# Gate and up products of a SwiGLU as seven half-size block products, with weight sums made by adding transfers

## The chip, the cores and the metric

The kernel runs on one core of a Trainium2 chip. The metric is the device time of one launch, in microseconds (us). Before the change three runs took 2916.46, 2917.67 and 2917.93 us; the median is 2917.67 us. The engines are named as the profile names them: PE (TensorE matmuls), PEld (its weight loads), DVE (VectorE), ACT (ScalarE), POOL (GpSimd) and SP (SyncE, which here only issues transfers).

## The reference

One encoder layer on 512 tokens of width 2048. A token mixer is followed by a layer norm, then by the part that the change touches:

```
h = x * (1.0 + sc_f) + sh_f                                   # x: the normed first residual, 512 x 2048
y = (silu(h @ w_gate) * (h @ w_up)) @ w_down                  # w_gate, w_up: 2048 x 5632; w_down: 5632 x 2048
x = layer_norm(ALPHA * x + (1.0 + gt_f) * y, ln2_g, ln2_b)
```

All of it is float32.

## The kernel before

Activations that feed a product stand feature-major: 128 features on the partitions, 512 tokens along a row. Every float32 product is three passes in float32r. An operand is cut into hi (rounded by an ACT copy) and lo = x - hi (a DVE subtraction), and `mm3` issues hi*hi, hi*lo and lo*hi into one PSUM bank. A weight tile of 128 x 1024 therefore costs an ACT copy (`round_to`, L319) and a DVE subtraction (`split_to`, L331). Five raw tiles (NRAW) and four hi/lo pairs (NW) are in rotation; the weights come from DRAM as one stream of such tiles in the order of use, loaded by SP.

The second half of the program, in order:

- The products with w_out give y, token tile by token tile for the last 512 columns. DVE makes the residual z in SBUF (`t0_0` to `t3_3`) and its statistics. `finish1(t)` norms a token tile, transposes it on PE (bank `zt`), scales it on ACT to h (tile `h2`), and DVE writes hi and lo of h (`m_hi`, `m_lo`).
- 44 feature tiles f of 128 features each. `gate_up` takes for each f a gate and an up product over 16 feature tiles of h: 16 x 3 matmuls of 512 columns each. The first feature tile is cut in two halves of 256 tokens, so that the last token tile can be normed meanwhile.
- After each part of four feature tiles, `down` multiplies the part before with w_down and DVE adds the result to `yacc`, which begins as ALPHA (z g + b) made on POOL (`base_side`).
- The last part goes by token tile, with the second layer norm behind it.

The order is written out by hand in each engine's own program order. Generators in `side` add the small work, one step for every 12 matmuls. Each engine runs its rows in order and waits where an operand is not there.

Of the kernel before, what the change touches and what calls it, by code (L numbers as in the profile page):

```python
# [13 lines left out]
"""  # L14
# [14 lines left out]
P = 128  # L29
D = 2048  # L30
# [26 lines left out]
NHEAP = 38  # L57
NSMALL = 14
# [12 lines left out]
def stream_keys():  # L71
    """The weight tiles in the order in which the products use them."""
# [28 lines left out]
    def gu(p):  # L101
        return [(g, f, i) for f in range(p * PART, p * PART + PART) for g in ("gate", "up") for i in range(2)]

    def down(p):
        return [("down", f, c) for c in range(4) for f in range(p * PART, p * PART + PART, 2)]

    ks += gu(0)
    for p in range(1, NPART):
        ks += gu(p) + down(p - 1)
# [3 lines left out]
    ks += [k for k in down(NPART - 1) if not k[2]] + stay  # L113
    return ks
# [3 lines left out]
def layer_kernel(ctx, tc, ws, wa, wada, xt, x, cin, bada, lbl, ghg, gcq, gckv, ln1c, lnrow, ident, lvm, dist, out):  # L118
# [6 lines left out]
    hp = ctx.enter_context(tc.tile_pool(name="heap", bufs=NHEAP))  # L125
# [6 lines left out]

    def big(name, dt=FR):
        return bp.tile([P, 4, T], dt, name=name, tag="big")
# [4 lines left out]
    # ---------------------------------------------------------------- constants  # L139
# [18 lines left out]
    # cond = silu(c) on every partition  # L158
# [64 lines left out]
    keys = stream_keys()  # L223
# [25 lines left out]
    class Stream:  # L249
        def __init__(self):  # L250
# [20 lines left out]
        def load_to(self, e):  # L271
            """Load at least up to this entry, and as far as the room reaches."""
            while self.ndma < len(entries):
                kind = entries[self.ndma]
                pool, most = self.room(kind)
                if self.ndma >= e and sum(self.room(entries[n])[0] == pool for n in self.raw) >= most:
                    break
# [6 lines left out]
                if kind[0] == "w":  # L284
                    nc.sync.dma_start(r, ws[kind[1]])
# [10 lines left out]
        def round_to(self, goal):  # L296
            """Take the adaLN products, round the weight tiles to hi, up to this entry of the stream."""
            while self.nhi <= min(goal, len(entries) - 1):
                e = self.nhi
                self.load_to(e + 1)  # L300
                kind = entries[e]
# [4 lines left out]
                else:  # L306
                    r = self.raw[e]
                    key = keys[kind[1]] if kind[0] == "w" else kind
# [16 lines left out]
        def split_to(self, goal):  # L325
            """The rests lo = w - hi, up to this entry."""
            self.round_to(goal)
            while self.nlo <= min(goal, len(entries) - 1):
# [10 lines left out]
        def get(self, *key, ahead=2):  # L339
            """A weight tile; the next ones that pass through are prepared ahead."""  # L340
            at = place_of["w", keys.index(key)]
            goals = [at]
            for e in range(at + 1, len(entries)):
                if len(goals) > ahead:
                    break
                if entries[e][0] == "w" and keys[entries[e][1]] not in self.held:
                    goals.append(e)
            if len(goals) <= ahead and not any(e[0] == "w" and keys[e[1]] not in self.held for e in entries[at + 1:]):
                goals.append(len(entries) - 1)
# [3 lines left out]
            return self.ready.pop(entries[at])  # L353

    W = Stream()

    # ---------------------------------------------------------------- h = x (1 + sc_m) + sh_m, its narrow projections
# [13 lines left out]
    def keep(key, ps):  # L371
        """Partial sums over the first features leave the banks."""
# [23 lines left out]
    def lower_bounds():  # L396
        """softmax over depth, cumsum - p0"""
# [17 lines left out]
    for k in range(KD):  # L415
# [37 lines left out]
        if k in (1, 2):  # L453
            # values of two token tiles over the first features
# [12 lines left out]
    # ---------------------------------------------------------------- rms of c_q and c_kv, spilled for the attention  # L467
# [29 lines left out]
    # ---------------------------------------------------------------- the indexer: scores and the 128 largest per query  # L497
# [5 lines left out]
    def key_side(t):  # L503
        """Index keys on both halves of the partitions; index weights token-major."""
# [13 lines left out]
    def index_queries(ps, h):  # L518
        """hi and lo of a head's index queries, one on each half of the rows, so that one product takes both."""
# [65 lines left out]
    # ---------------------------------------------------------------- token-major projections v, silu(g) for four heads  # L585
# [38 lines left out]
    def plus(res, ps, part):  # L624
        """res = ps + part"""
# [124 lines left out]
    # ---------------------------------------------------------------- sigmoid gates of the merge, spilled  # L750
# [56 lines left out]
    for j in range(4, KD):  # L807
        if j == 12:
# [3 lines left out]
            # the first 128 tokens unsplit: latent queries of two heads, latent keys  # L812
# [7 lines left out]
    # ---------------------------------------------------------------- attention: values of all heads, token-major  # L820
    # hi and lo of a head side by side, so that one product takes both
# [15 lines left out]
    # head pipeline: latent queries of head h, softmax of head h-1, values of head h-2  # L837
# [14 lines left out]
    def at_scores(h):  # L852
        """The products of a head's scores, up to the last query tile and then that; its softmax."""
# [66 lines left out]
    # y_a comes back while the last heads run; its products fill the end of the head pipeline  # L920
# [95 lines left out]
    # the residual gates scale the columns of w_out and w_down before these are split  # L1016
# [10 lines left out]
    # tiles that stay: the end of w_out and of w_down is taken token tile by token tile  # L1027
    def hold_out():
        return [(heap("wohi", FR), heap("wolo", FR)) for _ in range(2)]
# [4 lines left out]
    last_w = {}  # L1034

    def hold_down(f, c):
        def place():
            if c not in last_w:
                last_w[c] = (big(f"wdhi{c}"), big(f"wdlo{c}"))
            n = f - (NF - PART)  # L1040
            return [tuple(t[:, n + i] for t in last_w[c]) for i in range(2)]
        return place

    for c in range(1, 4):
        for f in range(NF - PART, NF, 2):
            W.held["down", f, c] = hold_down(f, c)

    # ---------------------------------------------------------------- merged = sig(ga) (y_a w_pa) + sig(gb) (y_b w_pb)
# [13 lines left out]
    del yb_hi, yb_lo, sa, sb  # L1062

# [335 lines left out]
```

## Time and profile before

| | |
|---|---|
| median of three runs | 2917.67 us |
| profiled execution: first to last instruction | 2914.7 us (the page gives no other time of it) |
| PE busy | 2874.3 us, 99% |
| DVE, ACT, POOL busy | 1664.9, 865.0, 382.3 us |
| end of the w_out products, start of gate and up | 1455.6 us |
| bytes moved by transfers | 407.46 MB, 140 GB/s on the mean |

The profile page sums each engine's busy time; a chain of waits follows the work that ended last back to the start; window tables give the same sums for one stretch. Matmuls overlap their neighbours, so the rate of PE is read from how far apart a run of them starts and not from the length of one.

### The profile page before, as it was taken

The numbers are of one execution on the slowest core, as the hardware profiler recorded it, in microseconds if no ns is written. First come the engines' busy times: TensorE is split into PE (matmuls) and PEld (weight loads), VectorE is DVE, ScalarE is ACT, GpSimd is POOL, SyncE is SP. The second block draws the span as 40 slices with busy tenths as digits, with TensorE's granted clock in tenths as the row PEclk, the third lists the DMA queues.
The fourth block names the chain that finished last, engine by engine and source line by source line (L and its number), as shares of the span: only waits on it lengthen the run. The fifth ranks groups of instructions, "written<-read, shape, count | busy, mean of one in ns | idle before, by whom it ended". The sixth has DMA issues, their size and how long they took to land.

```text
span 2914.7 us, 33709 instructions
## 1 busy us (share of the span) xinstructions
PE 2874.3 (99%) x13226; PEld 2391.8 (82%) x13226; DVE 1664.9 (57%) x2429; ACT 865.0 (30%) x1276; POOL 382.3 (13%) x435
## 2 busy tenths in 40 slices
PE   8999999999999999999999999999999999999997
PEld 6878888888888888888888888888888888888885
DVE  7877777778834876456643534244343524344358
ACT  4334342333223554222332222222222222222221
POOL 1011223332012443000062000000000000000003
PEclk9999999999999999999999999999999999999998
DMA  9866455557952124444233322332332233232341
GB/s 387 329 203 190 154 170 175 177 174 261 315 194 95 51 73 169 149 137 130 75 121 101 102 96 92 101 100 88 102 100 96 93 102 99 89 101 97 105 132 65
DMA packets 116049, 407.46 MB, mean 140 GB/s; under 512 B 14225, under 2 KB 14529, under 8 KB 112817
## 3 DMA queue, kind: packets, MB, share of 16 engines
q1 hardware_dynamic: 104690, 369.35, 37.7%
q0 software_dynamic: 10912, 35.64, 3.8%
q8 instruction: 104, 1.70, 0.2%
q14 instruction: 55, 0.45, 0.1%
q10 hardware_dynamic: 288, 0.31, 0.0%
HBM read 386.62 MB, written 16.27 MB: 138 GB/s over the span
## 4 chain that ended last, share of the span: by engine, by line
PE 94%; DVE 3%; DMA 1%; issue 1%; ACT 0%; POOL 0%; SPq 0%; DVEq 0%; POOLq 0%; ACTq 0%
PE gate L204 16%; PE up L204 16%; PE dn L204 16%; PE y L204 6%; PE gb L204 6%; PE ga L204 6%; PE qb L204 3%; PE pb L204 3%; PE g L204 3%; PE v L204 3%; PE pa L204 2%; PE early L204 2%; PE s L204 2%; PE a L204 1%; PE q L204 1%; PE f L204 1%
## 5 line engine op out<-in xcount | busy, mean ns | idle before, releaser
L331 DVE TENSOR_TENSOR wlo<-raw,whi 128x1024 fp32r<-128x1024 f32 (+1 forms) x486 | 597.2, 1251 | 474.4 <-ACT whi L319 470.2
L319 ACT ACTIVATE whi<-raw 128x1024 fp32r<-128x1024 f32 (+1 forms) x486 | 498.7, 1047 | 514.0 <-DVE raw L1022 241.3
L204 PE MATMUL gate<-mhi,wlo 128*128 128x512 f32 (+1 forms) x720 | 276.8, 384 | 0.0
L204 PE MATMUL up<-mhi,wlo 128*128 128x512 f32 (+1 forms) x720 | 276.8, 384 | 0.0
L204 PE MATMUL gate<-mlo,whi 128*128 128x512 f32 (+1 forms) x720 | 276.7, 384 | 0.0
L204 PE MATMUL gate<-mhi,whi 128*128 128x512 f32 (+1 forms) x720 | 276.7, 384 | 0.0
L204 PE MATMUL up<-mlo,whi 128*128 128x512 f32 (+1 forms) x720 | 276.7, 384 | 0.0
L204 PE MATMUL up<-mhi,whi 128*128 128x512 f32 (+1 forms) x720 | 276.7, 384 | 0.0
L204 PE MATMUL dn<-whi,gthi 128*128 128x512 f32 x656 | 255.2, 389 | 0.0
L204 PE MATMUL dn<-wlo,gthi 128*128 128x512 f32 x656 | 255.2, 389 | 0.0
L204 PE MATMUL dn<-whi,gtlo 128*128 128x512 f32 x656 | 255.2, 389 | 0.0
L1209 DVE TENSOR_TENSOR t<-t,dn 128x512 f32<-128x512 f32 x160 | 106.5, 684 | 141.2 <-PE dn L204 140.2
L1190 DVE TENSOR_TENSOR silu<-silu,up 128x512 f32<-128x512 f32 x43 | 29.6, 687 | 271.3 <-PE up L204 271.3
L1253 POOL DMA_DIRECT2D l<-in_lnrow x8 | 4.3, 542 | 1299.0 <-PE dn L204 1212.4
L204 PEld LDWEIGHTS gate<-mlo,whi 128*128 128x128 f32 x720 | 135.3, 188 | 26.9
L204 PEld LDWEIGHTS gate<-mhi,whi 128*128 128x128 f32 x720 | 135.3, 188 | 26.8
L204 PEld LDWEIGHTS up<-mlo,whi 128*128 128x128 f32 x720 | 135.3, 188 | 26.8
L204 PEld LDWEIGHTS up<-mhi,whi 128*128 128x128 f32 x720 | 135.3, 188 | 26.8
L204 PEld LDWEIGHTS gate<-mhi,wlo 128*128 128x128 f32 x720 | 135.3, 188 | 26.8
L204 PEld LDWEIGHTS up<-mhi,wlo 128*128 128x128 f32 x720 | 135.3, 188 | 26.8
L204 PEld LDWEIGHTS dn<-whi,gthi 128*128 128x128 f32 x656 | 123.1, 188 | 25.6
L204 PEld LDWEIGHTS dn<-wlo,gthi 128*128 128x128 f32 x656 | 123.1, 188 | 25.6
(349 smaller groups left out, 5672.2 us busy)
## 6 DMA issues: line engine op xcount, KB each, us to landing
raw<-in_ws SPq DMA_DIRECT2D x480, 512.0 KB, 3.9
raw<-in_wada SPq DMA_DIRECT2D x128, 512.0 KB, 4.9
rawb<-in_wada SPq DMA_DIRECT2D x22, 1024.0 KB, 12.1
raws<-in_wada SPq DMA_DIRECT2D x40, 256.0 KB, 6.3
d_gate<-sgate POOLq DMA_DIRECT2D x32, 256.0 KB, 3.0
raw<-in_wa SPq DMA_DIRECT2D x16, 384.0 KB, 10.0
raws<-in_xt SPq DMA_DIRECT2D x16, 256.0 KB, 10.3
spa<-d_gate POOLq DMA_DIRECT2D x16, 256.0 KB, 3.1
```

What stands on the lines that cost most here:

```text
L204: mmul(*a, **k)
L319: nc.scalar.activation(hi, src, AF.Copy)
L331: nc.vector.tensor_sub(lo, src, hi.bitcast(FT))
L1190: nc.vector.tensor_mul(s, s, ps)
L1209: nc.vector.tensor_add(yacc[t][c], yacc[t][c], ps)
L1253: nc.gpsimd.dma_start(rows2[n][c], lnrow[2 + n][:, c * T:c * T + T].to_broadcast([P, T]))
```

## The change

Gate and up become block products. The weight matrix is cut into four blocks (two halves of the features f, two halves of the 2048 inputs), h into four (two halves of the inputs, two of the tokens). A pair of feature tiles p and p + 22 of one kind (a "quad", 44 in all) is computed by seven products of half size in place of eight, in the Winograd form. Each is 8 x 3 matmuls of 256 columns (`product`). Three of them use plain blocks of h, four use sums of blocks: R5, R7, R6, R4.

- The sums of h are made once: `block_sums` adds or subtracts on DVE, `put` writes hi by ACT and lo by DVE. `sums_side` does this for R7, R6 and R4, R5 goes into `m_hi` and `m_lo`. The order of the first products is changed so that four plain ones run first.
- The sums of weights are made by transfers that add what they bring to what lies in the SBUF tile (`accum_op=OP.add`), issued by POOL: four for each quad, beside four plain loads by SP. Each state of a raw tile is split by ACT and DVE for its product (`prepare`, three steps ahead of PE): seven splits where there were four.
- The results are combined out of PSUM by ACT copies and DVE adds (`use`), and silu(gate) * up goes to DRAM (`d_g`).
- w_down is a stage of its own behind all gate and up products; its activations come back from DRAM and are split (`g_tiles`). z goes to DRAM as well (`d_z`), comes back for the first norm of the last columns, and again for `base_side`, which now runs beside w_down.

```
-    def gate_up(p, skip=0):
...
-                        mm3(ps, whi[:, w], wlo[:, w], *mh(k), k == 0, k == KD - 1)
...
+SEVEN = ("p1", "q5", "p2", "q7", "r6", "q4", "p3")
...
+    seq = [(0, "p1"), (1, "p1"), (0, "p2"), (1, "p2")]
+    seq += [(n, i) for n in range(2) for i in SEVEN if i not in ("p1", "p2")]
+    seq += [(n, i) for n in range(2, len(QUADS)) for i in SEVEN]
...
+        for step, what in ((s - 4, "F1"), (s - 3, "F3"), (s - 2, "+F1"), (s - 1, "Z"), (s + 2, "Y")):
...
+    BLOCK = {"F1": (1, 0), "F3": (0, 0), "Z": (0, 1), "Y": (1, 1), "+F1": (1, 1)}
+    OF = {"q5": "F1", "r6": "F1", "p1": "F3", "q7": "F3", "p2": "Z", "p3": "Z", "q4": "Y"}
...
+    def fetch_for(step):
+        for n, what in fetch.pop(step, ()):
+            if what[0] == "+":
+                nc.gpsimd.dma_start(raws[n, what[1:]], block(n, what), accum_op=OP.add)
...
+            nc.sync.dma_start(r, block(n, what))
...
+    def prepare(step):
+        fetch_for(step)
...
+        split(r, hi, lo)
+        if i == "q5":
+            nc.gpsimd.dma_start(r, block(n, "F3"), accum_op=OP.add)
+        elif i == "p1":
+            nc.gpsimd.dma_start(r, block(n, "F1"), accum_op=OP.add)
+        if i == ("p2" if n > 1 else "q5"):
+            nc.gpsimd.dma_start(raws[n, "Z"], raws[n, "F1"], accum_op=OP.add)
...
+    def put(v, hi, lo):
+        nc.scalar.activation(hi, v, AF.Copy)
+        nc.vector.tensor_sub(lo, v, hi.bitcast(FT))
...
+        for c in range(2):
+            r = passing("r5")
+            nc.vector.tensor_sub(r, hraw[t - 2, c], hraw[t, c])
+            put(r, m_hi[c][:, :, s], m_lo[c][:, :, s])
+        yield "R5"
...
+    def product(step):
+        for k in range(8):
+            mm3(ps, whi[:, w], wlo[:, w], *factor(i, k), fresh and k == 0, k == 7, f=mmul, skip_group_check=True)
...
+    for step in range(4, len(seq)):
+            prepare(step + 3)
+        product(step)
+        use(step)
```

DVE where gate and up begin: before, `h` is the last token tile of h on its way into `mhi` and `mlo`, and `wlo` are weight rests.

```order
L1106 TENSOR_TENSOR mlo0_9438<-h2_11801,mhi0_9437 128x4x128
L1105 CAST mhi1_9723<-h2_11808 128x4x128
L1106 TENSOR_TENSOR mlo1_9724<-h2_11808,mhi1_9723 128x4x128
L1105 CAST mhi2_10009<-h2_11837 128x4x128
L1106 TENSOR_TENSOR mlo2_10010<-h2_11837,mhi2_10009 128x4x128
L1105 CAST mhi3_10295<-h2_11844 128x4x128
L1106 TENSOR_TENSOR mlo3_10296<-h2_11844,mhi3_10295 128x4x128
L331 TENSOR_TENSOR wlo_11940<-raw_11364,whi_11939 128x1024
```

The same place on DVE now, from the last lo of R7 to the weight rest behind R4:

```order
L1142 TENSOR_TENSOR R7_1_11962<-h2_11898,R7_1_11962 128x4x128
L1157 TENSOR_TENSOR h2_11582<-h2_11893,h2_11582 128x512
L1157 TENSOR_TENSOR h2_11589<-h2_11898,h2_11589 128x512
L1142 TENSOR_TENSOR R6_0_11963<-h2row_11410,R6_0_11963 128x4x128
L1142 TENSOR_TENSOR R6_1_11964<-h2row_11410,R6_1_11964 128x4x128
L1142 TENSOR_TENSOR R6_0_11963<-h2_11582,R6_0_11963 128x4x128
L1142 TENSOR_TENSOR R6_1_11964<-h2_11589,R6_1_11964 128x4x128
L273 TENSOR_TENSOR wlo_11986<-raw_11806,whi_11985 128x1024
L1160 TENSOR_TENSOR h2_11546<-h2_11546,h2_11582 128x512
L1160 TENSOR_TENSOR h2_11553<-h2_11553,h2_11589 128x512
L1142 TENSOR_TENSOR R4_0_11965<-h2row_11410,R4_0_11965 128x4x128
```

Behind the last token tile DVE had only weight rests; now the sums of h stand between them, six rows for each of R7, R6 and R4.

POOL in the first 100 us of gate and up, before: the rows of the second layer norm's base.

```order
L1165 DMA ln0_3_12026<-in_lnrow 128x512
L1166 TENSOR_SCALAR ln0_3_12026<-ln0_3_12026 128x512
L1165 DMA ln1_3_12030<-in_lnrow 128x512
L1166 TENSOR_SCALAR ln1_3_12030<-ln1_3_12030 128x512
L1170 TENSOR_TENSOR t0_0_10711<-t0_0_10711,ln0_0_12023 128x512
L1171 TENSOR_TENSOR t0_0_10711<-t0_0_10711,ln1_0_12027 128x512
```

POOL there now, from the reload of the last token tile on: `raw<-in_ws` is an adding transfer, `raw<-raw` one from SBUF to SBUF.

```order
L1243 DMA z_11618<-d_z_10458 128x512
L1098 DMA xin_11622<-in_x 128x512
L1221 DMA raw_11624<-in_ws 128x1024
L1221 DMA raw_11626<-in_ws 128x1024
L1203 DMA raw_11632<-in_ws 128x1024
L1260 DMA d_z_10458<-xin_11622 128x512
L1219 DMA raw_11632<-in_ws 128x1024
L1223 DMA raw_11628<-raw_11632 128x1024
L1203 DMA raw_11916<-in_ws 128x1024
L1219 DMA raw_11916<-in_ws 128x1024
L1223 DMA raw_11630<-raw_11916 128x1024
```

POOL has nothing but transfers there now, and its queue carries the adding ones in the order of the program: L1203, L1221, L1219, L1223 for each quad.

## Rows read from the trace of the kernel before

**Rows 1.** The page's busy times: engine, us, share of the span, instructions.

```profile
PE 2874.3 (99%) x13226; PEld 2391.8 (82%) x13226; DVE 1664.9 (57%) x2429; ACT 865.0 (30%) x1276; POOL 382.3 (13%) x435
```

**Rows 2.** The page's chain that ended last, shares of the span by engine.

```profile
PE 94%; DVE 3%; DMA 1%; issue 1%; ACT 0%; POOL 0%; SPq 0%; DVEq 0%; POOLq 0%; ACTq 0%
```

**Rows 3.** Waits of PE, the longest: waited for, us in total, times, longest.

```profile
PE a L204 <- ACT hThi L436: 5.9, 1, 5.9
```

**Rows 4.** Window table: stretch, its us, busy us by engine, PEclk, DMA share, GB/s.

```profile
1455.60:1480.50 24.90, 24.90 (x210) 24.90 (x209) 14.37 (x23) 11.94 (x24) 9.44 (x9) 1.00 0.53 170
1480.50:2850.00 1369.50, 1369.50 (x6044) 1133.97 (x6043) 571.21 (x593) 309.46 (x347) 59.68 (x47) 1.00 0.31 99
2850.00:2914.00 64.00, 44.92 (x199) 36.86 (x197) 51.63 (x69) 10.13 (x16) 21.33 (x15) 0.89 0.21 74
```

**Rows 5.** Chain of waits from 1440 us on: start us, us, what.

```profile
1463.32 0.87 PE zt L1096 x8
...
1468.98 5.76 PE gate L204 x48
...
1480.50 10.91 PE gate L204 x48
1491.41 10.88 PE up L204 x48
```

**Rows 6.** Instructions by line, PE, by shape: count, busy us, mean ns.

```profile
L204 PE MATMUL gate<-mhi,whi 128*128 128x512 f32 x688 | 267.6, 389 | 0.0
L204 PE MATMUL gate<-mhi,whi 128*128 128x256 f32 x32 | 9.0, 283 | 0.0
```

**Rows 7.** Instructions by line, DVE, by shape.

```profile
L331 DVE TENSOR_TENSOR wlo<-raw,whi 128x1024 fp32r<-128x1024 f32 x260 | 315.4, 1251 | 362.2 <-ACT whi L319 358.6
L1209 DVE TENSOR_TENSOR t<-t,dn 128x512 f32<-128x512 f32 x160 | 106.5, 684 | 141.2 <-PE dn L204 140.2
L1022 DVE TENSOR_TENSOR raw<-raw,gtf 128x1024 f32<-128x1024 f32 x88 | 104.3, 1219 | 0.0
L1106 DVE TENSOR_TENSOR mlo<-h,mhi 128x512 fp32r<-128x512 f32 x16 | 11.4, 710 | 0.5
L690 DVE TENSOR_TENSOR ks<-kt,G 128x256 f32<-128x256 f32 x48 | 20.0, 418 | 0.0
```

**Rows 8.** Instructions by line, ACT, by shape.

```profile
L319 ACT ACTIVATE whi<-raw 128x1024 fp32r<-128x1024 f32 x260 | 267.3, 1055 | 337.8 <-DVE raw L1022 174.4 <-PE dn L204 129.4 <-issue 29.4
L246 ACT ACTIVATE gthi<-silu 128x512 fp32r<-128x512 f32 x44 | 27.8, 632 | 369.7 <-DVE silu L1190 366.1 <-DVE silu L1234 3.7
```

**Rows 9.** Timeline of DVE and ACT, last token tile: start us, us, line, what.

```profile
1456.75 0.68 DVE L1150 SCALAR_TENSOR_TENSOR t<-xin,y 128x512 f32<-128x512 f32 x1
...
1458.82 0.16 DVE L1073 RECIPROCAL mv<-mv 128x1 f32<-128x1 f32 x1 [0.36 <-ACT mv L1072]
1459.02 0.21 DVE L1074 TENSOR_SCALAR mv<-mv 128x1 f32<-128x1 f32 x1
1459.15 1.91 DVE L1088 TENSOR_SCALAR t<-t,mv 128x512 f32<-128x512 f32 x4
...
1461.50 5.69 ACT L1103 ACTIVATE h<-zt,colB,colA 128x128 f32<-128x128 f32 x16 [0.81 <-PE zt L1096]
```

**Rows 10.** Transfers by line: count, KB each, median us from issue to landing.

```profile
raw<-in_ws SPq DMA_DIRECT2D x480, 512.0 KB, 3.9
d_gate<-sgate POOLq DMA_DIRECT2D x32, 256.0 KB, 3.0
gtm<-d_row POOLq DMA_DIRECT2D x1, 1024.0 KB, 6.7
gtf<-d_row POOLq DMA_DIRECT2D x1, 1024.0 KB, 5.1
```

**Rows 11.** Transfer queue q1 in 0:100 and 300:700 us: packets, MB, share of 16 engines.

```profile
q1 hardware_dynamic: 8801, 35.61, 90.1%
...
q1 hardware_dynamic: 17543, 63.91, 48.9%
```

More of the change, by code (lines that the diff above doesn't have):

```diff
@@ L99, in stream_keys, with down_keys, down @@
                 ks.append(stay.pop(0))
[L101 to L109, printed above, removed]
+    return ks
+def down_keys():
+    def down(n):
+        return [("down", f, c) for c in range(4) for f in (2 * n, 2 * n + NP2)]
+    ks = [k for n in range(NPART - 1) for k in down(n)]
     stay = [k for k in down(NPART - 1) if k[2]]
@@ L112, in stream_keys, with block_keys @@
         ks.insert(ks.index(k) + 1, stay.pop(0))
-    ks += [k for k in down(NPART - 1) if not k[2]] + stay
-    return ks
+    return ks + [k for k in down(NPART - 1) if not k[2]] + stay
+SEVEN = ("p1", "q5", "p2", "q7", "r6", "q4", "p3")
+NP2 = NF // 2
+def block_keys():
+    return [(kind, f, i) for f in range(NF) for kind in ("gate", "up") for i in range(2)]
+def stream_keys():
+    return first_keys() + block_keys() + down_keys()
 @with_exitstack
@@ L271, in load_to @@
         def load_to(self, e):
-            while self.ndma < len(entries):
-                kind = entries[self.ndma]
+            while self.ndma < len(self.entries):
+                kind = self.entries[self.ndma]
                 pool, most = self.room(kind)
-                if self.ndma >= e and sum(self.room(entries[n])[0] == pool for n in self.raw) >= most:
+                if self.ndma >= e and sum(self.room(self.entries[n])[0] == pool for n in self.raw) >= most:
                     break
@@ L1028, in hold_out @@
     def hold_out():
-        return [(heap("wohi", FR), heap("wolo", FR)) for _ in range(2)]
+        return [(passing("wohi", FR), passing("wolo", FR)) for _ in range(2)]
     for i in OUT_STAY:
         W.held["out", 3, i] = hold_out
[L1034 to L1046, printed above, removed]
     m_hi, m_lo = [], []
@@ L1151, in layer_kernel, with sums_side @@
+            nc.vector.scalar_tensor_tensor(z, z, ALPHA, ps, op0=OP.mult, op1=OP.add)
             nc.vector.bn_stats(st1[t][:, c * 6:c * 6 + 6], z)
+            nc.gpsimd.dma_start(d_z[t, c], z)
             if c == 3:
                 side.add(t, finish1(t))
-    del banks, xs, wl, w, ps, gtm
+    del banks, xs, wl, w, ps, z, gtm
     W.scale.clear()
-    yacc = tt
+    sums = {}
+    last_sums = block_sums(3)
+    def sums_side():
+        for i in ("R7", "R6", "R4"):
+            sums[i] = [rp.tile([P, 4, T], FR, name=f"{i}_{c}", tag="sum") for c in range(2)]
+        for i, t, c in (("R7", 2, 0), ("R6", 0, 0), ("R4", 0, 2)):
+            if i != "R7":
+                next(last_sums)
+            for dt in range(2):
+                for dc in range(2):
+                    put(hraw.pop((t + dt, c + dc)) if i == "R4" else hraw[t + dt, c + dc],
+                        sums[i][dc][:, :, dt * P:dt * P + P], sums[i][dc][:, :, (dt + 2) * P:(dt + 3) * P])
+            if i != "R7":
+                for at in [at for at in hraw if (at[0] >= 2 if i == "R6" else True)]:
+                    del hraw[at]
+            yield
@@ new lines, in product @@
+    def product(step):
+        n, i = seq[step]
+        whi, wlo = pairs.pop(step)
+        name = STARTS[i]
+        fresh = i in ("p1", "q5", "q7", "r6")
+        if fresh:
+            acc[n, name] = bank(name)
+        ps = acc[n, name][:, :H]
+        for k in range(8):
+            w = slice(k * P, k * P + P)
+            mm3(ps, whi[:, w], wlo[:, w], *factor(i, k), fresh and k == 0, k == 7, f=mmul, skip_group_check=True)
+            if step < 16 and k % 4 == 3:
+                side.step()
@@ new lines, in layer_kernel, with g_tiles @@
+    for step in range(4):
+        prepare(step + 3)
+        product(step)
+        use(step)
+    for t in range(NT):
+        side.drain(t)
+    assert [next(last_sums) for _ in range(2)] == ["R5", "R7"]
+    xp.release()
+    rp = tc.alloc_tile_pool(name="sums", bufs=6, side="right", reuse_waits="tile")
+    side.add(0, sums_side())
+    side.step()
+    side.step()
+    dkeys = down_keys()
+    W2 = Stream(dkeys, [("w", i) for i in range(len(dkeys))])
+    gtf = None
+    gT = {}
+    def g_tiles(n):
+        his, los = big(f"gthi{n}"), big(f"gtlo{n}")
+        for j in range(4):
+            f = 2 * n + j % 2 + j // 2 * NP2
+            r = heap("graw")
+            nc.sync.dma_start(r, d_g[f])
+            split(r, his[:, j], los[:, j])
+            gT[f] = (his[:, j], los[:, j])
@@ new lines, in layer_kernel @@
+    for step in range(4, len(seq)):
+        if step + 3 < len(seq):
+            prepare(step + 3)
+        product(step)
+        use(step)
+        if step == 8:
+            side.drain(0)
+            assert not hraw
+        if step == 16:
+            gtf = gate_row(1, "gtf")
+            W2.scale["down"] = scaled(gtf)
+        if step == len(seq) - 6:
+            for a in (m_hi, m_lo):
+                a[0] = a[1] = None
+            g_tiles(0)
+            W = W2
+        if step >= len(seq) - 4 and step < len(seq) - 1:
+            W.round_to(step - len(seq) + 4)
+            W.split_to(step - len(seq) + 4)
@@ new lines, in layer_kernel, with hold_down, place @@
+    del m_hi, m_lo
+    sums.clear()
+    mh = None
+    rp.release()
+    yp = ctx.enter_context(tc.tile_pool(name="sumsout", bufs=6, side="right", reuse_waits="tile"))
+    yacc = [yp.tile([P, 4, T], FT, name=f"yacc{t}", tag="y") for t in range(NT)]
+    last_w = {}
+    def hold_down(f, c):
+        def place():
+            if c not in last_w:
+                new = (lambda name: yp.tile([P, 4, T], FR, name=name, tag="y")) if c == 1 else big
+                last_w[c] = (new(f"wdhi{c}"), new(f"wdlo{c}"))
+            n = 2 * (f > NP2)
+            return [tuple(t[:, n + i] for t in last_w[c]) for i in range(2)]
+        return place
```

308 lines of the change are left out of this document (199 added, 109 removed).

## The prediction

> **What bounds the kernel now.** I read the busy times first, then the chain of waits, then PE's own waits, then the window table. PE is busy 2874.3 of 2914.7 us [rows 1] and the chain that ended last is 94% PE [rows 2]. The longest wait of PE is 5.9 us, once, near the start [rows 3]. From 1455.6 us, where gate and up begin, to 2850 us PE is busy all the time at the full granted clock, 1.00 or 2.4 GHz, while DVE is busy for 571 of 1369.5 us, ACT for 309, and transfers hold 0.31 of their engines [rows 4]. So time in this half is matmul time; what is added to the other engines costs nothing until one of them, or a transfer, is late for PE.
>
> The rate of PE is read from the chain: 48 matmuls of 512 columns take 10.88 us, 226.7 ns each; 48 of 256 columns take 5.76 us, 120.0 ns each, back to back [rows 5]. Half the columns cost 53% of the time: each matmul carries 13 ns that its width does not change.
>
> **Term 1: the matmuls.** Before, gate and up are 688 x 6 = 4128 matmuls of 512 columns and 32 x 6 = 192 of 256 (one of the six kinds in each width: [rows 6]): 4128 x 0.2267 + 192 x 0.120 = 935.8 + 23.0 = 958.8 us. Now there are 44 quads x 7 products x 24 = 7392 matmuls of 256 columns: 308 products of 2.88 us, 887.0 us, a quad 20.16 us. The gain is 71.8 us. One product in eight would be worth 120 us at an unchanged price per column; 48 us of that go to the narrower matmul. The w_down matmuls and the products up to y are the same in number and width.
>
> The Trainium skill (TensorE: Matmul & The Clock Gate, Back-to-back issue gap) gives columns / 2.4 + 2.5 ns, 109.2 and 215.8 ns; by it the gain would be 105 us. The trace is 11 ns above it at either width [rows 5], so the rows decide.
>
> **Term 2: where gate and up begin.** The first four products use plain blocks of h. The next ones need R5, R7, R6 and R4 for all tokens, and these follow from the last token tile, which is known only when y has ended. PE's own work from the end of y to the first product that uses R4 is 7 products x 2.88 + 2 x 0.87 for the transposes [rows 5] = 21.9 us. DVE's rows in the same stretch, counted in its order: 28 of 512 columns for the sums of h (14 adds or subtractions, 14 rests lo) x 0.71 = 19.9; 4 for the last columns of h, 2.8; 5 weight rests x 1.25 = 6.3 [rows 7]; the norm of the last tile 4.3, from 1456.75 to 1461.06 [rows 9]; one of 256 columns 0.4. That is 33.7 us, so PE waits at least 11.8. DVE also waits itself: for an ACT copy of 0.63 [rows 8] at five places where a sum is fresh, 3.2 us, and for the transposes with half of ACT's 5.69 us [rows 9], about 3 us. Stretch 39.9, wait 18 us. Bounds: 12 if DVE never waits; 30 if the first adding transfer also lands late, up to 6.7 us [rows 10], and the granted clock falls in the gaps, as in the last 64 us, where PE is busy for 45 us and the clock is 0.89 [rows 4].
>
> **Term 3: the steady quads.** ACT: seven copies x 1.055 plus about 2.5 for results = 10 of 20.16 us. DVE: seven rests x 1.25 plus five to eight rows of results x 0.42 to 0.7 = 11 to 12.5 us [rows 7, 8]. Both fit. A raw tile is split three steps (8.6 us) ahead of its product and the split takes 2.3 us, so 6.3 us are left for lateness. The cover is gone when the transfers are late, and these are the unknown: no transfer of the trace adds.
>
> What an adding transfer of 512 KB costs: not less than a plain one, since it brings the same bytes. A plain one costs the 16 engines 1.33 us where they are full (35.61 MB in 90.1% of 100 us) to 1.60 us (63.91 MB in 48.9% of 400 us) [rows 11], and lands in 3.9 us [rows 10]. An adding one reads the tile too, twice the reading: then 2.7 to 3.2 us, and it lands as the nearest rows of twice the bytes, 5.1 and 6.7 us [rows 10]. If read, read and write do not overlap, three times: 4.0 to 4.8 us. A quad has 4 plain loads, 4 adding ones and on the mean half a unit for `d_g`: 8.5 units = 11.3 to 13.6 us at once the price; 12.5 units = 16.6 to 20.0 at twice; 16.5 units = 21.9 to 26.4 at three times. PE needs 20.16. I take twice: term 3 is then 0, with little to spare.
>
> The add itself is said to be free but to need two reads for each write, half the rate of a copy (Trainium skill, Collectives: The Full Stack, The bandwidth ceiling). By that a quad is the 16.6 to 20.0 us above and the sum stays; no run here shows an adding transfer yet.
>
> Lateness: the longest chain is q5's split, F1 += F3's block, Z += F1, and then the load of the next Z, which waits for the tile that Z += F1 has read. With L for the landing of an adding transfer it is 2.9 + 2L + 0.6 + 4.0, and the next p2 is split 23 us after the first split began: nothing is late up to L = 7.7 us. POOL's and SP's queues are in order: behind a late Z += F1 stand the next +F1 on POOL, and on SP the loads of Y and F1.
>
> **Term 4: w_down alone.** For 10.88 us of PE, DVE has two scalings x 1.22, two rests x 1.25, four adds x 0.68 [rows 7], in sum 7.7, plus 0.7 for splitting activations and about 1.6 while `base_side` runs: 10.0 of 10.88. Four pairs in rotation cover a local excess. I take 2 us, bounds 0 and 10. z and g through DRAM are 256 KB pieces that land in 3.0 us [rows 10], asked for well before use; nothing.
>
> **Sum.** 2914.7 - 71.8 + 18 + 0 + 2 = 2862.9 us of span. The median of the runs stands 3.0 us above that span; with it 2866 us.
>
> **Rivals.**
> - Transfers bind (slower). The place is the steady quad; it decides once an adding transfer takes over 3.2 to 3.5 us of the engines, (20.16 - 4.5 x 1.60 or 1.33) / 4. At three times the price a quad takes 21.9 to 26.4 us, middle 24.2: 44 x 4.0 = 178 us more, 3044 us (2943 to 3140). For it: twice the price already uses 82 to 99% of the time, and transfers that read and write one tile may not overlap. Against it: the engines moved 395 GB/s in the first 100 us, and a quad at twice the price asks for 325.
> - Landing at the edge. Transfers fit, but L is about 8.2 us because four queue behind plain loads; 2 x 0.5 = 1 us for each quad, 44 us, 2910 us. For it: landing times of loads vary with the load of the queue. Against it: 6.7 us is the longest of the POOL queue's rows for twice the bytes.
> - The start costs only DVE's minimum of 12 us and w_down nothing: 2858 us, the same side, the low end of the forecast's own range.
>
> **How the numbers follow.** Forecast 0.60, with a range of its own of 2858 to 2886 (terms 2 and 4 at both ends: -6 - 2 and +12 + 8). The edge 0.14, from there to 2923. Transfers bind 0.24, a quarter of it under 2990. Below 2858: 0.02, and the range goes 8 us under it, since the last 64 us, with PE busy for 45 [rows 4], could also gain. A measurement of this kernel tells about 0.2%, 5.8 us, from no change: 2911.8 to 2923.5 counts as the same. Faster: 0.60 + 0.02 + 0.11 of the edge = 0.73. Same: 0.03 of the edge + 0.01 of the bound case = 0.04. Slower: 0.23. The range 2850 to 2990 holds 0.60 + 0.14 + 0.06 = 0.80 and a little.
>
> **What would show it.** Right: the lines of A, B, D and E with 7392 matmuls of 256 columns and 2.88 us for each 24; PE's longest waits for DVE's rests of R5, R7, R6 and R4, some 18 us in all near 1470 us; no other wait of PE over 1 us; adding transfers landing in 5 to 7 us; a DMA share of 0.8 to 1.0 in gate and up, 0.31 before. Wrong: PE waiting in every quad for weight rests that follow the adding transfers (L1203, L1219, L1221, L1223 of the changed kernel), landing times over 8 us, or a gap of PE in w_down with DVE busy throughout.

## The result and the profile after

The changed kernel takes 2932.54 us (median of four runs, 2930.63 to 2935.63), the kernel before 2917.8 us beside it: a ratio of 1.0054, interval 1.0040 to 1.0068. It is slower by half a per cent where 2866 us, faster by 1.8%, was forecast. The time lies inside the range of 2850 to 2990, but not where the forecast put its weight (2858 to 2886), and on the other side of the kernel before. The profiled execution has a span of 2931.3 us, against 2914.7 before.

The page's busy times after, as in [rows 1]:

```profile
PE 2835.0 (97%) x16298; PEld 2488.6 (85%) x16298; DVE 1931.3 (66%) x2843; ACT 1064.7 (36%) x1594; POOL 557.4 (19%) x655
```

PE has less to do than before (2835 us, 2874.3 before), but 96 us of the span are idle where 40 were. So the matmuls did get cheaper, and something else ate it. The chain that ended last, 94% PE in [rows 2], now reads:

```profile
DMA 17%; PE 13%; issue 9%; DVE 6%; ACT 2%; POOL 1%; SPq 0%; POOLq 0%; ACTq 0%; DVEq 0%
```

These shares add up to 48% only: the chain can be followed back from the end as far as 1496 us and no further, so it says nothing of the first half. From there on the page puts it on the transfers into `raw` (12% and 3%) and on `dn`, the matmuls of w_down (11%): in the steady quads it runs through the weights and not through PE. What each stage lost is read from a window table (columns as in [rows 4]): the start of gate and up, the steady quads, and w_down in four pieces.

```profile
1467.20:1510.00 42.80, 30.54 (x204) 29.39 (x203) 34.75 (x54) 26.63 (x48) 4.05 (x5) 0.80 0.53 116
1510.00:2392.00 882.00, 867.43 (x7208) 860.97 (x7208) 475.60 (x586) 374.21 (x495) 152.37 (x174) 1.00 0.89 221
2392.00:2480.00 88.00, 85.02 (x366) 69.25 (x365) 56.89 (x64) 28.62 (x40) 14.73 (x13) 0.98 0.43 138
2480.00:2680.00 200.00, 176.40 (x731) 141.87 (x730) 144.79 (x167) 42.22 (x48) 56.03 (x49) 0.94 0.40 128
2680.00:2880.00 200.00, 200.00 (x884) 165.48 (x883) 151.44 (x180) 52.52 (x63) 4.33 (x8) 1.00 0.39 125
2880.00:2931.30 51.30, 31.58 (x138) 25.53 (x136) 40.86 (x54) 6.56 (x11) 20.83 (x14) 0.85 0.24 82
```

The first row holds 16 transposes (1.74 us) and 188 matmuls, worth 22.6 us at 120 ns: 18.5 us lost. The second holds the other 7204, worth 864.5 of its 882.0: 17.5 lost. The fourth is the one to look at: 731 matmuls in 200 us, 153 short of the 884 that the row below has in the same time, 34 us. While POOL is busy (56 us, then 4.3) PE stands, and it stops standing when POOL does. The matmuls themselves are as forecast in number, and their rows, as in [rows 6], show the width:

```profile
L237 PE MATMUL A<-mhi,whi 128*128 128x256 f32 x704 | 200.6, 285 | 1.0 <-ACT e L1323 0.9
L239 PE MATMUL D<-R,wlo 128*128 128x256 f32 x704 | 197.6, 281 | 0.0
```

Put beside the kernel before, stage by stage:

| us | forecast | measured |
|---|---|---|
| up to gate and up (1455.6, now 1467.2) | 0 | +11.6 |
| term 1, 7392 matmuls, counted at 120.0 ns, for 958.8 us | -71.8 | -71.8 |
| term 2, start | +18 | +18.5 |
| term 3, steady quads | 0 | +17.5 |
| term 4, w_down and the end (498.6, now 539.3) | +2 | +40.7 |
| sum | -51.8 | +16.5 |

(498.6 is 2914.7 - 1455.6 - 958.8 - 1.7 for the transposes.) The row of term 1 takes the forecast's own 120.0 ns for every matmul, so only the count in it is measured. The 3168 matmuls on the sums R start 117 ns apart (median; 118.3 on the mean), which wins some 5 us; they are hidden in the row of term 3. By the distances of matmul starts alone PE loses 23 us in the steady quads, 21 at q4 and 2 at p2. What PE waits for longest, as in [rows 3]:

```profile
PE dn L229 <- ACT whi L347: 16.9, 5, 8.1
PE D L237 <- ACT y L1337: 15.3, 22, 2.1
PE dn L229 <- DVE wlo L359: 9.6, 8, 1.6
PE a L229 <- ACT hThi L464: 7.9, 1, 7.9
PE zt L1121 <- DVE z L1112: 6.2, 1, 6.2
```

The first and third row are w_down (`dn`): 26.5 us of waits for weights. The second is in the steady quads: q4, which adds into bank D, waits in 22 quads for ACT's copy `y` of q7's result out of that bank. No wait of that list is for a rest that follows an adding transfer. The transfers, as in [rows 10]:

```profile
raw<-in_ws SPq DMA_DIRECT2D x480, 512.0 KB, 4.3
raw<-in_ws POOLq DMA_DIRECT2D x132, 512.0 KB, 6.9
raw<-raw POOLq DMA_DIRECT2D x44, 512.0 KB, 6.4
zrel<-d_z POOLq DMA_DIRECT2D x16, 256.0 KB, 3.0
```

Adding transfers land in 6.9 and 6.4 us, as forecast.

### The profile page after: what moved, and what is told of

Its sections match the earlier page's. It is cut to its first block, busy times and chain, and to the rows that moved or that the text cites. A ratio compares the mean times of both kernels' runs of the same rounds, so it can differ in the third digit from the quotient of the medians.

```text
span 2931.3 us, 41521 instructions
## 1 busy us (share of the span) xinstructions
PE 2835.0 (97%) x16298; PEld 2488.6 (85%) x16298; DVE 1931.3 (66%) x2843; ACT 1064.7 (36%) x1594; POOL 557.4 (19%) x655
## 5 line engine op out<-in xcount | busy, mean ns | idle before, releaser
L273 DVE TENSOR_TENSOR wlo<-raw,whi 128x1024 fp32r<-128x1024 f32 x308 | 376.6, 1225 | 406.3 <-ACT whi L272 405.5
L359 DVE TENSOR_TENSOR wlo<-raw,whi 128x1024 fp32r<-128x1024 f32 (+1 forms) x310 | 382.4, 1244 | 134.1 <-ACT whi L347 130.7
L272 ACT ACTIVATE whi<-raw 128x1024 fp32r<-128x1024 f32 x308 | 325.4, 1057 | 393.2 <-DMA raw<-in_ws 194.9
L237 PE MATMUL D<-R,whi 128*128 128x256 f32 x704 | 201.2, 286 | 15.7 <-ACT y L1337 15.3
L237 PE MATMUL B<-mhi,whi 128*128 128x256 f32 x704 | 200.3, 284 | 3.4 <-ACT mhi L1141 3.4
L237 PE MATMUL A<-mhi,whi 128*128 128x256 f32 x704 | 200.6, 285 | 1.0 <-ACT e L1323 0.9
L238 PE MATMUL B<-mlo,whi 128*128 128x256 f32 x704 | 200.2, 284 | 0.1
L239 PE MATMUL B<-mhi,wlo 128*128 128x256 f32 x704 | 200.0, 284 | 0.0
L239 PE MATMUL A<-mhi,wlo 128*128 128x256 f32 x704 | 199.7, 284 | 0.0
L238 PE MATMUL A<-mlo,whi 128*128 128x256 f32 x704 | 199.7, 284 | 0.0
L238 PE MATMUL D<-R,whi 128*128 128x256 f32 x704 | 197.7, 281 | 0.0
```

The source lines that it names most:

```text
L237: f(ps, ahi, bhi, start=first, stop=False, **k)
L238: f(ps, ahi, blo, start=False, stop=False, **k)
L239: f(ps, alo, bhi, start=False, stop=last, **k)
L272: nc.scalar.activation(hi, src, AF.Copy)
L273: engine.tensor_sub(lo, src, hi.bitcast(FT))
L359: nc.vector.tensor_sub(lo, src, hi.bitcast(FT))
```

## The experiments

### w_down: base_side in smaller steps, and without it

DVE in w_down, from its timeline (start us, us, line, what, in brackets the wait ahead of it and for what):

```profile
2531.63 0.68 DVE L1455 TENSOR_TENSOR yacc<-yacc,zrel 128x512 f32<-128x512 f32 x1
2532.24 1.28 DVE L1475 TENSOR_TENSOR yacc<-yacc,dn 128x512 f32<-128x512 f32 x2
2541.02 0.55 DVE L1450 TENSOR_SCALAR zrel<-zrel,mv 128x512 f32<-128x512 f32 x1 [7.50 <-DMA zrel<-d_z]
2541.48 0.68 DVE L1475 TENSOR_TENSOR yacc<-yacc,dn 128x512 f32<-128x512 f32 x1
2542.08 4.20 DVE L1050 TENSOR_TENSOR raw<-raw,gtf 128x1024 f32<-128x1024 f32 x2
```

`base_side` asks for z and puts the norm of z (L1450) on DVE in one and the same step. The reload stands on POOL behind the scaling of the rows `ln`, which waits for its own transfers, so DVE waits 7.5 us, and behind it in DVE's order stands the scaling of the next w_down weights (L1050). ACT and PE then wait for these. The scaling itself takes 2.1 us each there, beside POOL's product, and 1.2 elsewhere. Two theories: the order (head of the line), or simply too much work on DVE. The edit, shortened (the rows `ln` are asked for ahead in the same way):

```diff
-                nc.gpsimd.dma_start(z, d_z[t, c])
...
+            if n + 1 < len(places):
+                z_load(n + 1)
...
                 nc.vector.tensor_scalar(z, z, mv1[t][:, 0:1], ...)
                 yield
                 nc.gpsimd.tensor_mul(z, z, rows[c][0])
                 nc.gpsimd.tensor_add(z, z, rows[c][1])
                 yield
+                yield
+                yield
                 nc.vector.tensor_add(yacc[t][:, c], yacc[t][:, c], z)
```

> The changed kernel with base_side cut into other steps: the reload of z and the rows of ln are asked for one piece ahead, DVE's norm of z comes a step after the reload and DVE's add to yacc three steps (8 us) behind POOL's product and sum. No work is added or left out. Theory H (head of the line): in 2480 to 2680 us DVE stands 27.5 us for reloads of z and 9.5 us for POOL, each in front of the scaling of w_down, and PE loses 34 us there; with the steps apart the PE waits for whi and wlo in w_down fall from 26.5 to under 4 us, the stage from 539 to 500-505 us, and the time to about 2896. Theory W (DVE has too much to do once w_down has no gate and up beside it, 10.0 of 10.88 us, and POOL and DVE slow each other): the waits move to wlo and stay over 20 us, 2920 or more.

Measured: 2896.66 us, ratio to the kernel before 0.9930 (0.9918 to 0.9943). The same window as above, and DVE's longest waits from 2440 to 2680 us, first after, then in this run:

```profile
2480.00:2680.00 200.00, 200.00 (x884) 165.69 (x883) 165.70 (x196) 48.72 (x57) 54.98 (x49) 1.00 0.47 144
```

```profile
DVE zrel L1450 <- DMA zrel<-d_z: 29.7, 6, 8.7
DVE yacc L1475 <- PE dn L229: 13.2, 9, 2.0
DVE yacc L1455 <- POOL zrel L1453: 11.1, 7, 1.6
```

```profile
DVE yacc L1496 <- PE dn L229: 28.1, 20, 2.0
DVE gtlo L273 <- ACT gthi L272: 10.7, 6, 1.8
```

PE now does 884 matmuls in the 200 us, and DVE is busy for 0.83 of the time. It no longer waits for a transfer or for POOL in these rows, only for PE and ACT. POOL is as busy as before, and the scaling of w_down beside it costs DVE as much (whole run, as in [rows 7]; after, then this run):

```profile
L1050 DVE TENSOR_TENSOR raw<-raw,gtf 128x1024 f32<-128x1024 f32 x88 | 116.2, 1361 | 0.0
```

```profile
L1050 DVE TENSOR_TENSOR raw<-raw,gtf 128x1024 f32<-128x1024 f32 x88 | 115.5, 1353 | 0.0
```

So it was the order, and theory W falls in both its parts, the amount of work and the slowing beside POOL.

The other run leaves base_side out (`side.add(0, base_side())` and the drain are gone):

> The changed kernel without base_side: ALPHA times the first norm's result and bias are left out of what is summed in yacc, so the result lacks them. Theory H and theory W agree here: PE no longer waits in w_down, the stage takes 479 us of matmuls and 20 of tail, about 500, and the time is 2893. If over 10 us of waits stay, w_down alone is what costs them (term 4 by its scalings and rests) and base_side only part of it.

Measured: 2892.95 us (0.9916; 0.9902 to 0.9929). By the medians leaving all of it out gives 3.7 us more than spreading it, but the intervals of the two ratios overlap, and the stage itself hardly differs: w_down takes 501.3 us without it, 501.8 spread, 539.3 as it was.

### The steady quads: ACT's copies, and plain transfers

ACT in one steady quad after, and PE there:

```profile
1887.97 1.05 ACT L272 ACTIVATE whi<-raw 128x1024 fp32r<-128x1024 f32 x1
1893.72 1.06 ACT L272 ACTIVATE whi<-raw 128x1024 fp32r<-128x1024 f32 x1 [4.70 <-DMA raw<-raw]
1894.69 0.36 ACT L1337 ACTIVATE y<-D 128x256 f32<-128x256 f32 x1
```

```profile
1894.01 0.28 PE L237 MATMUL E<-R,whi 128*128 128x256 f32 x1
1895.11 0.38 PE L237 MATMUL D<-R,whi 128*128 128x256 f32 x1 [0.58 <-ACT y L1337]
```

q7 had ended at 1891.5, but its copy out of bank D stands on ACT behind the hi copy of p3's weights, and that waits 4.7 us for Z += F1 to land. Only q7's copy was moved first:

```diff
+        late = seq[step][1] == "q7"
-        if step + 3 < len(seq):
+        if step + 3 < len(seq) and not late:
             prepare(step + 3)
         product(step)
         use(step)
+        if late:
+            prepare(step + 3)
```

> The changed kernel, with the split for p3 (ACT's hi copy, DVE's rest and what is fetched with them) issued behind q7's product and its ACT copy of the result (y<-D), and not ahead of them. Theory Q (ACT's queue): in the steady quads ACT's copy of q7's result stands behind the hi copy of p3's weights, which waits for the transfer inside SBUF (3 to 5 us a quad); q4 starts in the same bank D and waits for the copy. With the order turned the waits of PE at q4, 28 of them with 21 us in all, are gone: 2932 - 20 = 2912. Theory T (the transfers themselves are late): the wait moves to p3, whose weights come as late as before: 2925 to 2932, with PE waiting for wlo at B in its place.

Measured: 2927.63 us (1.0031; 1.0020 to 1.0043). That is the time of theory T, but not its wait: the waits at q4 are gone but for one of 1.2 us, and 11.4 us at p2, 7 waits for the copy `e` of p1's result (L1323), took their place, the same thing at the other bank. So both were moved (`late = ... in ("p1", "q7")`):

> The changed kernel with ACT's copies of p1's and of q7's result ahead of the split that stood in front of them (so far only q7's was moved: the waits of PE at q4 went, and 11.4 us of waits at p2, in bank A for p1's copy, came in their place, 7 of them). Theory Q: with both moved no product waits for a copy; of the 21 us that PE lost at q4 in the steady quads under 4 are left, gate and up take 924.8 - 18 = 907 us and the time is 2914. Theory T (late transfers): as much waiting at other products, for wlo of the weights whose split now comes later, gate and up at 917 to 925.

Measured: 2924.44 us (1.0021; 1.0012 to 1.0030). In the steady quads no product waits for a copy any more; 3.4 us of waits are left, six at p3 for its rest (7.1 us by the distances of starts). Gate and up take 909.2 us, 15.6 less, near what theory Q gave. The median is only 8 us lower: in the profiled execution w_down lost 3 us more and y began 1.7 us later.

What the adding itself costs, by leaving it out (no `accum_op` in the four calls):

> The changed kernel with the 176 adding transfers as plain ones of the same size in the same places, so that sums of weights are not made (the result lacks them). It prices the adding: landing 6.9 and 6.4 us now, near 4.3 as plain; DMA share in the steady quads 0.89 now, and if an adding transfer costs the engines two plain ones, 8.5 / 12.5 of it, 0.61. Theory Q: hi copies no longer wait for transfers, so ACT's copies of results are in time although they stand behind them; the waits at q4 go and gate and up take 905. Theory T: the same. If waits at q4 stay over 10 us, neither holds, and ACT's own work makes them.

Measured: 2910.27 us (0.9974; 0.9965 to 0.9984), gate and up 901.4 us, 23.4 less. The waits at q4 went from 15.3 us to one of 2.1. POOL's queue from 1600 to 2300 us (packets, MB, share of 16 engines), after and then in this run:

```profile
q0 software_dynamic: 19669, 71.66, 57.6%
```

```profile
q0 software_dynamic: 19985, 72.79, 30.1%
```

With 136 and 139 transfers in these 700 us, an adding one takes the 16 engines 0.576 x 700 / 136 = 2.96 us, a plain one 1.52: the ratio is 1.95. The forecast had taken twice the plain price, 2.7 to 3.2. They landed in 4.0 and 4.2 us as plain ones. By the rule that an add needs two reads for each write and so half a copy's rate (Trainium skill, Collectives: The Full Stack, The bandwidth ceiling) the ratio is 2; this trace agrees.

### The first half: where the tiles stand

The instructions ahead of gate and up are the same in both kernels, yet y began 11.1 us later (1287.2, 1276.1 before). The distance of matmul starts shows most of it. In a product `pb` after, whose moving operand is a tile of the pool heap (PE's timeline):

```profile
1209.96 0.40 PE L229 MATMUL pb<-ybhi,wlo 128*128 128x512 f32 x1
...
1213.46 0.40 PE L229 MATMUL pb<-ybhi,wlo 128*128 128x512 f32 x1
```

15 matmuls in 3.50 us, 233.3 ns each, where [rows 5] have 226.7. The change moved heap to the right side of SBUF and made another pool 128 bytes larger. Before, all large tiles had one rest by 2048 bytes; after, the tiles of heap and of the pools that follow it lie 32 bytes short of that of the weight tiles and the big tiles. The edit sets some bytes aside at the right end:

```diff
+    ap = ctx.enter_context(tc.tile_pool(name="align", bufs=1, side="right"))
+    ap.tile([P, 8], FT, name="align")
     hp = tc.alloc_tile_pool(name="heap", bufs=NHEAP, side="right")
```

> The changed kernel with 32 bytes more per partition set aside at the right end of SBUF, so that every tile of the pools heap, stay, pass, sums and sumsout stands on a multiple of 64 bytes, as before the change, and no longer 32 bytes off. Nothing else moves. Theory P (placement): the 512-column matmuls whose moving operand lies in those tiles (qidx, uv, qb, pa, pb) start 227 ns apart again and not 231 to 235 ns; y starts at about 1278 us and not 1287, and the time falls by 9 us to about 2923. The 256-column matmuls that read the sums R start 117 ns apart now, those that read m_hi and m_lo 120; if that too is placement, they go to 120 and 3168 x 3 ns = 9 us come back on the other side, 2932. Theory N (the first half differs by the start or by noise): y starts at 1287 us as now and the time stays at 2932.

> As the run before, but the 32 bytes are given back when the pool heap is released, so that only the first 1200 us or so have their tiles on multiples of 64 bytes, and the sums R lie 32 bytes off as in the changed kernel. Theory P: 2923 us, with R's matmuls 117 ns apart. Theory N: 2932 us.

Measured: 2929.1 us (1.0036; 1.0024 to 1.0049) and 2930.89 us (1.0049; 1.0035 to 1.0063). Theory P as it was put fell: the matmuls on heap stayed at 231 to 235 ns in both. In the first run R's matmuls went to 113 to 114 ns and not to 120, but PE's waits at q4 grew from 15.3 to 23.6 us, and gate and up took 923.2 us where they had taken 924.8. But the kernel before with 32 bytes in front of heap (the same two lines, on the left side) became slow:

> The kernel before the change with one tile of 32 bytes per partition in front of the pool heap, so that heap's tiles lie 32 bytes off a multiple of 64. Theory P: some 1400 to 1500 matmuls of 512 columns ahead of y go from 227 to 231-235 ns, y starts 9 us later, and what reads heap tiles in the rest (the held weights of the last w_out and w_down columns) adds under 1 us: 2927 us, slower by 0.3%. Theory N: 2918 us, no change.

Measured: 2938.28 us, 1.0071 (1.0058 to 1.0084): 20 us and not 9, because the w_down matmuls, whose stationary operand lies in heap there, went to 233 ns too; before this shift they take 227. y began 6.7 us later, and the other 13 us are some 2100 matmuls of w_down at 6 ns each. So placement counts, for either operand, but a multiple of 64 is not what is wanted. Two more paddings, 96 and 2016 bytes:

> The changed kernel with 96 bytes per partition set aside at the right end of SBUF. The tiles of heap, pass, stay, sums and sumsout then stand on multiples of 128 bytes, but 1920 bytes behind the multiples of 2048 on which the weight tiles and the big tiles stand; before the change all of them had the same rest by 2048. What the first runs left: 32 bytes of padding (rest 1984) leaves the 512-column matmuls with a heap operand at 231 to 235 ns, so a multiple of 64 is not what they want, and the 256-column ones on R went from 117 to 113 ns. Theory A (absolute place, multiples of 128): the 512-column ones return to 227 ns and R's to 120; y starts near 1278 plus a spread of the start of up to 4 us. Theory C (place of one operand against the other, by 2048): they stay at 233 and R's are at 113 ns or below. Time 2923 to 2932 by either.

> As the run before, with 2016 bytes set aside: all tiles have one and the same rest by 2048, as before the change. Both theories: 512-column matmuls with a heap operand at 227 ns, y earlier by 9 us; those of 256 columns on R at 120 ns like those on m_hi and m_lo, 3168 x 2.9 = 9 us more in gate and up unless they only fill what q4 waits for now. Time 2923 to 2933. Should the pitch stay at 233 in this run too, the place of tiles is not what makes it.

Measured: 2928.24 us (1.0042; 1.0028 to 1.0055) and 2923.37 us (1.0021; 1.0011 to 1.0030). The same product in the run with 2016 bytes:

```profile
1205.52 0.39 PE L231 MATMUL pb<-ybhi,whi 128*128 128x512 f32 x1
...
1210.28 0.39 PE L231 MATMUL pb<-ybhi,whi 128*128 128x512 f32 x1
```

21 in 4.76 us: 226.7 ns again. Median distance of starts in ns, by how many bytes the one operand lies short of the other's rest by 2048 (worked out from the order and sizes of the pools):

| short by | 512 columns, heap (`pb`, `qidx`) | 256 columns, R (`D`, `E`) |
|---|---|---|
| 0 (2016 set aside) | 227 | 120 |
| 32 (as changed) | 232 to 235 | 117 |
| 64 (32 set aside) | 233 to 235 | 113 to 114 |
| 128 (96 set aside) | 232 | 119 |

Theory C holds for the 512-column matmuls. For the narrow ones it missed: 113 ns or below was forecast for 96 bytes, and it is 119. At 32 and 64 bytes apart they are faster than at 0, at 128 hardly. Why the place counts, no run shows. In the four runs with heap at rest 0 y begins at 1280.8 to 1283.4 us, in the others of the changed kernel at 1287.2 to 1291.8: 8 us on the mean. The 6 us from there to the 1276.1 of the kernel before stay open; 2 to 3 of them are in PE's first wait for h (7.8 to 9.1 us in these four runs, 5.9 in [rows 3]).

### The start

> The changed kernel with five weight rests at the start of gate and up (the steps 4 to 8) made on POOL in place of DVE; four of them stand on DVE ahead of the last row of R4. Theory S (DVE's sum of rows bounds the start): R4 comes 4 x 1.22 = 4.9 us earlier, up to 8.7 with the 3.8 us that DVE stands for ACT before one of them, and PE's 18.8 us of loss from 1467 to 1510 us fall to 10-14; time 2924 to 2928. Theory U (other waits, of PE for the norm of the last token tile and of DVE for ACT, bound it, or POOL's rests of 2.5 us come too late for their products): no gain, 2930 to 2935.

```diff
-        split(r, hi, lo)
+        split(r, hi, lo, nc.gpsimd if 4 <= step <= 8 else nc.vector)
```

Measured: 2940.3 us (1.0077; 1.0064 to 1.0090), 8 us worse than the changed kernel (its profiled execution 4 us). POOL's first rest there, and DVE's norm of the last token tile at the same time:

```profile
1481.95 2.33 POOL L273 TENSOR_TENSOR wlo<-raw,whi 128x1024 fp32r<-128x1024 f32 x1 [3.98 <-ACT whi L272]
```

```profile
1481.92 2.65 DVE L1112 TENSOR_SCALAR z<-z,mv 128x512 f32<-128x512 f32 x1
```

One quarter of the norm takes 2.65 us where it took 0.5, since it stands while POOL's rest runs. PE's wait for that norm grew from 6.2 to 8.4 us, and over the first 16 products the distances of matmul starts add up to 27.7 us lost where they had 18.8. Theory U holds, though the time lies above its 2930 to 2935: what is taken from DVE is given back as long as POOL does it beside DVE. Whether DVE's rows alone bound the start, this run can't tell.

### Together, and what holds it then

> What the runs so far point to, together: base_side in smaller steps (-36 us measured), both copies first (-18 by theory Q), heap's tiles on the same rest by 2048 as weights and big tiles (-9 us ahead of y), and behind that the sums R 64 bytes off it (their 256-column matmuls 113 ns apart and not 117: 3168 x 4 ns = -12 us). 2932 - 75 = 2857 if they add, 2875 if theory T holds for the copies.

Here 2016 bytes are set aside while heap lives and 32 behind it, so that R lies 64 bytes short. Measured: 2878.8 us, ratio 0.9868 (0.9854 to 0.9881): faster than both kernels, by 1.3% and 1.8%, but 22 us short of the sum. y begins at 1283.4, w_down takes 506 us, R's matmuls are 113 ns apart. Yet a steady quad takes 20.20 us (from the first E of one quad to that of the next, mean), and 20.20 also with both copies moved alone, where R's matmuls were 117 apart: the 12 us expected of R's place did not come. What PE waits for longest:

```profile
PE B L241 <- DVE wlo L275: 10.0, 17, 0.8
PE a L231 <- ACT hThi L466: 8.7, 1, 8.7
```

The wait has moved to p3's rest, whose weights come through both chained adding transfers. Two runs on that; the first with all transfers plain, the second with

```diff
-            nc.gpsimd.dma_start(raws[n, "Z"], raws[n, "F1"], accum_op=OP.add)
+            nc.gpsimd.dma_start(raws[n, "Z"], block(n, "F1"), accum_op=OP.add)
```

> The combined version with the 176 adding transfers as plain ones in the same places (the sums of weights are not made, the result lacks them). In the combined version a steady quad takes 20.23 us, as with R's matmuls 117 ns apart (20.21 us), though its products are worth 4 x 2.88 + 3 x 2.71 = 19.65 us; PE waits 17 us at p3 for the rest of its weights. If transfers hold the quad at 20.2 (either theory below), it falls to 19.65 to 19.75 and the time to 2855 to 2859. If matmuls or DVE hold it, it stays at 20.2 and 2879.

Measured: 2851.08 us (0.9772; 0.9755 to 0.9788), 19.68 us a quad, no loss of PE in the steady quads. In the run above with plain transfers a quad took 20.03 us, 20.20 with the copies moved and the adding kept. So adding holds the quad.

> The combined version, with the fourth adding transfer of a quad (Z += F1, from tile to tile) taking the same bytes out of DRAM, from F1's plain block: still an adding transfer of 512 KB, but it no longer waits for the one before it to have landed in F1 (the sums for p3 are therefore others than the product wants). Theory L (a chain of two landings): q5's split, F1 += 6.8 us, Z += F1 6.9 us and 6 us to the next q5's split close a ring of 19.8 to 20.2 us; with one landing out of it a quad takes 19.65 to 19.75 us and the time is 2855 to 2860. Theory R (rate: 16 engines at 0.89 to 0.95 of their time): nothing changes, 20.2 us and 2879.

Measured: 2911.23 us (0.9982; 0.9972 to 0.9991), 21.08 us a quad, slower. Neither theory said so. Loads in the steady quads of the combined version and then of this run (1600 to 2300 us):

```profile
raw<-in_ws SPq DMA_DIRECT2D x139, 512.0 KB, 5.0
```

```profile
raw<-in_ws SPq DMA_DIRECT2D x134, 512.0 KB, 7.2
```

What PE waits for longest in it:

```profile
PE A L239 <- ACT e L1328: 25.0, 19, 1.4
PE B L241 <- DVE wlo L275: 10.6, 17, 0.8
```

The two adding transfers are no longer one behind the other, and the plain loads land 2.2 us later. By the distances of starts PE loses 28 us ahead of p2, in 20 of the quads, where it waits for ACT's copy `e` of p1's result, and 26 us ahead of and within q5; that the later loads make these losses is argued and not shown. The chain is therefore not the only bound, and the mean rate is not either (the DMA share fell from 0.89 to 0.85). Which of them sets the 20.2 us stays open.

## Why the prediction was wrong

The steps that failed are term 4, which decided the sign, term 3, and one that the sum did not have.

- **Term 1** held. 24 matmuls of p or q5 take 2.88 us. R's products take 2.84, by the place of their tiles (2.88 with the same rest by 2048).
- **Term 2** held in size (18 forecast, 18.5 lost), which is in part luck, since its parts are others: 6.2 us are PE's wait for the norm of the last token tile, ahead of the transposes, some 6 us are waits for R5's hi, for a result's copy and for R's rest, and for what is left the window shows a granted clock of 0.80. That DVE's sum of rows bounds it is not shown; taking five rests off DVE gave nothing, with POOL as the helper.
- **Term 3** failed at "nothing is late up to L = 7.7 us". L was 6.4 to 6.9, and what was late first was ACT's copy of a result, in ACT's order behind a hi copy that waits for a landing. The prediction named what is queued behind a waiting transfer on POOL and SP, and not what is queued behind the waiting hi copy on ACT. The steady quads lost 23 us by the distances of starts (17.5 against 120.0 ns for all): 15.6 came back with the copies moved, and 7.1 stayed at p3, whose rest was late although L was 6.4 to 6.5. All of it, 23.4 us, came back without the adding.
- **Term 4** failed and decided the sign: 2 us, bounds 0 and 10, against 40.7. The step "10.0 of 10.88. Four pairs in rotation cover a local excess" counted work and no waits. `base_side` added a wait of DVE for a transfer and for POOL, in front of the scaling of weights, and "z and g through DRAM ... asked for well before use; nothing" was wrong: it is asked for in the same step. Asking earlier, with the same work, took w_down from 539.3 to 501.8 us, 3.2 above the 498.6 of before: for the work alone the 2 us were about right.
- **Not in the sum at all**: the side of the pool heap. I read the change for its instructions and not for its addresses; about 8 of the 11.6 us.
- **The rivals.** Transfers bind: at the price measured, 2.96 us, the share was 0.89 and it does not decide; but leaving out the adding is worth 22 us here and 28 in the combined version, through lateness. (The 395 GB/s set against this rival is the rate while the engines are full; the mean of those 100 us is 358.) Landing at the edge: the right kind of price (23 us measured, 44 forecast, by landings), mostly through ACT's order and not through the weights. Neither named w_down.

The forecast said that w_down with a gap of PE and DVE busy throughout would show it wrong. The gap was there, with DVE standing.

## What to carry to other kernels

Where a change puts an instruction that waits into an engine's order, list what stands behind it on that engine, for every engine: work sums do not show it. Ask for a reload a step or more before the instruction that needs it, and issue the reading of a result ahead of anything that waits for a transfer. A change of pools moves addresses; compare the distance of matmul starts in stages that nobody meant to change.

## Unexpected in the hardware

- The distance of matmul starts depends on how the two operands' tiles lie to one another in SBUF: 227 ns at the same rest by 2048 bytes, 232 to 235 ns at 32 to 128 bytes apart for 512 columns; 120 ns against 113 to 119 ns for 256 columns. What makes it is not shown. That the narrow ones on `m_hi` and `m_lo` would also fall to 113 with their weights 64 bytes off was not tried. The Trainium skill (SBUF — State Buffer, Who interferes with whom) has only the pair of ports shared by DVE and POOL as a place of contention, and PE's two read ports, for the moving operand and for the weights, as independent. The runs with shifted pools show that the place of the one operand against the other counts all the same.
- For that shared pair the run with rests on POOL agrees: DVE's row of 0.54 us took 2.65 beside a POOL subtraction, and one POOL rest 6.5 us beside DVE's rows where another took 2.3.
- Adding transfers of 512 KB: 2.96 us of 16 engines, 1.95 times a plain one, landing in 6.4 to 6.9 us against 4.0 to 4.2.
